# The first norm of a two-layer hybrid trunk: loads in order of need, the gain spread by products, and 22 unread products on TensorE ahead of the first transposes

## The chip, the cores and the metric

The kernel runs on one core of a Trainium2 chip. The metric is the device time of one execution in microseconds (us). The core has five instruction streams that run side by side and wait for each other by semaphores: TensorE (PE; its weight loads are shown as PEld), VectorE (DVE), ScalarE (ACT), GpSimd (POOL) and SyncE (SP), which here only issues transfers.

## What is computed

`x` has 1024 positions of 1024 channels in float32. Two layers follow each other, each with a mixer and a SwiGLU, and each of these sits between two RMS norms:

```python
def sandwich(x, g_pre, g_post, fn):
    return x + rmsnorm(fn(rmsnorm(x, g_pre)), g_post)

def even_mixer(t, layer_idx, w_in, lq1, lk1, lq2, lk2, subln, dw_w, dw_b, ln_g, ln_b, w_out, cos, sin):
    proj = t @ w_in
    y_a = diff_attention(proj[..., :3 * DIFF_WIDTH], layer_idx, lq1, lk1, lq2, lk2, subln, cos, sin)
    y_b = conformer_conv(proj[..., 3 * DIFF_WIDTH:], dw_w, dw_b, ln_g, ln_b)
    return jnp.concatenate([y_a, y_b], axis=-1) @ w_out
```

The change concerns the very start: `rmsnorm(x, l0_mix_pre)` of layer 0, the first of the projections behind it (the gated input of the convolution), and the scalar lambda of differential attention, which is made of four vectors of 64.

## The kernel before, in words

All large products are made in three terms of two rounded parts, high and low (`mm3`, lines 114 to 122): high by high, high by low, low by high, each a matmul with its own weight load. A weight unit is 128 by 1024. `unit` (L84 to L92) loads it into `raw`, ScalarE rounds it to `wh` (L89), and GpSimd subtracts to give `wl` (L91). `raw` has five buffers.

`first_norm` (L139 to L155) loads the eight blocks of 128 positions (`nt`, five buffers, L144), the gain as a transfer that repeats one line for all 128 partitions (`gpre`, L111, L150), and the first two weight units. For every block ScalarE sums the squares (`junk`, L106), GpSimd makes the inverse root (`rstd`, L97 and L98), VectorE multiplies block, root and gain (`nx`, L153), and `to_T` turns the block: eight transposes on TensorE in two groups of four (`tr`, two PSUM buffers, L181), each group rounded by ScalarE (`xt`, L183) and its low part split off by VectorE (L184). Four blocks make one half, 512 columns, of the transposed input `X`.

`conv` (L186 to L220) makes four chunks of 128 channels. For every chunk and half it forms two projections into one PSUM tile (`psc`, `proj_cm`, 24 matmuls of 512 columns each); ScalarE takes the sigmoid of the second, VectorE multiplies. Three of the eight pieces of the convolution are then made by ScalarE and GpSimd, five by VectorE (31 steps each, `psk`, L215 and L217). `qk0` makes queries and keys from the same `X` and stores them through memory. `lam` (L326 to L340) loads the four vectors, multiplies, sums, takes the exponential and scales one more gain (`sub8`).

In the program text `first_norm` comes first, then `lam`, then `conv` and `qk0`. The order in which each engine's instructions are issued is not that of the text: a scheduler places them by times that it simulates, and keeps the order fixed from then on. Transfers are all issued by SyncE in one queue in order; so is the work of ScalarE, VectorE and GpSimd.

```python
        for tb, r in enumerate(rows):
            xn = pool.tile([P, D], F32, tag="nx", name="nx", bufs=3)
            rs = self.sumsq(r)
            nc.vector.scalar_tensor_tensor(xn, r, rs, g, op0=ALU.mult, op1=ALU.mult)
            self.to_T(xn, X[tb // 4], tb % 4)
```

## Time and profile before

| | |
|---|---|
| median of 3 runs | 2328.14 us (2327.58 to 2334.51) |
| the profiled execution | 2332.52 us |
| its span, first to last instruction | 2330.1 us |
| mean granted TensorE clock | 0.968 |
| TensorE busy (matmul) | 2157.9 us, 93% of the span |
| VectorE, GpSimd, ScalarE busy | 1594.9, 1265.7, 945.2 us |
| transfers | 135 GB/s in the mean |

The profile is of one execution. Times in it count from its first instruction. The chain is the work that ended last, followed back from the end of the program: at each step to what released it. A bracket at the end of a timeline row is the time that the engine was idle before, and what ended it. A granted clock of 1.00 is TensorE's full 2.4 GHz, 0.5 is 1.2 GHz; it is recorded only from the first change on, so the pace of the products has to be looked at too in the first 30 us.

### The profile page before, as it was taken

Reading aid. Unit: us, or ns where it says so; the run is one execution under the profiler, and the core shown is the slowest. Engines: PE = TensorE matmul, PEld = TensorE weight load, DVE = VectorE, ACT = ScalarE, POOL = GpSimd, SP = SyncE. Lnnn points to the kernel's source line nnn. Section 1 sums busy time; section 2 is a strip of 40 time slices with the busy share of each in tenths; the row PEclk is TensorE's granted clock in tenths of the full one; section 3 lists DMA queues with packets and bytes.
Section 4 is the critical chain, followed back from the end, with each engine's and each line's share of the span. In section 5 each row is a group of like instructions: output and inputs, shape, how many; then the busy total and the mean of one; then the engine's idle time right before and its main releaser. Section 6 shows DMA issues by size and latency. Waiting matters only on the chain.

```text
span 2330.1 us, 27167 instructions
## 1 busy us (share of the span) xinstructions
PE 2157.9 (93%) x9684; PEld 1746.3 (75%) x9684; DVE 1594.9 (68%) x2175; ACT 945.2 (41%) x1413; POOL 1265.7 (54%) x740
## 2 busy tenths in 40 slices
PE   7999889898999999899969888999899999989987
PEld 5887677676788878687758767876688888878866
DVE  6859567689856865477884578656964444447788
ACT  5554555453222332333344346654532322234332
POOL 4997202134665556776644455421575656577674
PEclk9999999899999999899979999999999999999999
DMA  5234683243332343644542674324332323255354
GB/s 204 71 109 140 167 206 112 76 168 107 107 117 100 123 136 104 221 140 134 173 160 80 193 232 141 113 97 160 119 131 72 133 73 131 73 178 185 112 167 149
DMA packets 150662, 315.32 MB, mean 135 GB/s; under 512 B 20224, under 2 KB 43904, under 8 KB 150528
## 3 DMA queue, kind: packets, MB, share of 16 engines
q1 hardware_dynamic: 150528, 313.60, 41.4%
q8 instruction: 76, 1.25, 0.2%
q14 instruction: 58, 0.48, 0.1%
HBM read 214.39 MB, written 96.01 MB: 133 GB/s over the span
## 4 chain that ended last, share of the span: by engine, by line
PE 68%; DVE 16%; DMA 6%; issue 4%; ACT 3%; POOL 3%; SPq 0%; POOLq 0%; DVEq 0%; ACTq 0%
PE b L115 29%; PE psd L115 13%; PE psw L115 6%; PE psc L115 5%; PE psq L115 3%; PE po L115 2%; DVE hl L1253 2%; DVE acc L1271 2%; PE pss L1038 2%; PE trp L365 1%; POOL wl L1123 1%; DVE wt L1042 1%; PE pss L452 1%; DMA bm<-k_s 1%; PE psv L115 1%
## 5 line engine op out<-in xcount | busy, mean ns | idle before, releaser
L1123 POOL TENSOR_TENSOR wl<-raw,wh 128x1024 fp32r<-128x1024 f32 (+1 forms) x238 | 614.1, 2588 | 412.3 <-ACT wh L1121 399.7
L115 PE MATMUL b<-T,wh 128*128 128x512 f32 x1408 | 438.4, 392 | 2.2 <-DVE F L1172 2.2
L1121 ACT CAST wh<-raw 128x1024 fp32r<-128x1024 f32 (+1 forms) x238 | 241.9, 1023 | 433.0 <-PE b L115 251.7
L115 PE MATMUL b<-B,wh 128*128 128x512 f32 x1056 | 337.4, 400 | 15.0 <-DVE c L1163 10.5
L115 PEld LDWEIGHTS b<-T,wh 128*128 128x128 f32 x1408 | 263.8, 188 | 62.3 <-issue 2.8
L115 PE MATMUL b<-T,wl 128*128 128x512 f32 x704 | 276.4, 393 | 1.6 <-POOL wl L1123 1.6
L115 PE MATMUL psd<-wh,hh 128*128 128x512 f32 x616 | 240.6, 400 | 32.6 <-ACT hh L1252 18.9
L115 PEld LDWEIGHTS b<-B,wh 128*128 128x128 f32 x1056 | 203.0, 193 | 62.5 <-ACT B L1089 7.3
L115 PE MATMUL psd<-wl,hh 128*128 128x512 f32 x616 | 241.4, 396 | 0.0
L115 PE MATMUL psd<-wh,hl 128*128 128x512 f32 x616 | 235.2, 396 | 1.3 <-DVE hl L1253 1.3
L1271 DVE TENSOR_TENSOR acc<-acc,psd 128x512 f32<-128x512 f32 (+1 forms) x208 | 177.8, 884 | 60.1 <-PE psd L115 60.0
L115 PE MATMUL b<-B,wl 128*128 128x512 f32 x528 | 210.9, 400 | 3.6 <-POOL wl L1123 3.6
L115 PE MATMUL psw<-wh,jt 128*128 128x512 f32 x512 | 176.0, 410 | 16.0 <-ACT jt L488 9.3
L1172 DVE TENSOR_TENSOR p<-p,b 128x1024 f32<-128x1024 f32 (+1 forms) x88 | 83.5, 950 | 135.3 <-PE b L115 134.9
L1252 ACT CAST hh<-hr 128x1024 fp32r<-128x1024 f32 (+1 forms) x84 | 82.2, 979 | 223.8 <-PE psd L115 206.6
L115 PEld LDWEIGHTS psd<-wh,hh 128*128 128x128 f32 x616 | 117.2, 190 | 67.3 <-ACT hh L1252 23.9
L1253 DVE TENSOR_TENSOR hl<-hr,hh 128x1024 fp32r<-128x1024 f32 (+1 forms) x84 | 152.5, 1826 | 16.6 <-ACT hh L1252 16.6
L115 PEld LDWEIGHTS b<-T,wl 128*128 128x128 f32 x704 | 132.1, 188 | 32.7 <-POOL wl L1123 2.8
L91 POOL TENSOR_TENSOR wl<-raw,wh 128x1024 fp32r<-128x1024 f32 x48 | 122.2, 2558 | 58.4 <-ACT wh L89 58.4
L115 PEld LDWEIGHTS psd<-wh,hl 128*128 128x128 f32 x616 | 117.1, 190 | 28.9 <-DVE hl L1253 2.6
L115 PEld LDWEIGHTS psd<-wl,hh 128*128 128x128 f32 x616 | 117.5, 191 | 25.5
L1173 DVE TENSOR_TENSOR raw<-raw 128x1024 f32<-128x1024 f32 x66 | 106.7, 1617 | 41.3 <-POOL wl L1123 40.2
(386 smaller groups left out, 4314.4 us busy)
## 6 DMA issues: line engine op xcount, KB each, us to landing
raw<-in_l_gu_dram SPq DMA_DIRECT2D x96, 512.0 KB, 3.6
hr<-l_h_s SPq DMA_DIRECT2D x70, 512.0 KB, 4.1
raw<-in_l_dn_dram SPq DMA_DIRECT2D x48, 512.0 KB, 3.8
l_h_s<-F SPq DMA_DIRECT2D x66, 256.0 KB, 2.3
raw<-in_w_in_dram SPq DMA_DIRECT2D x27, 512.0 KB, 3.5
l_h_s<-c SPq DMA_DIRECT2D x44, 256.0 KB, 2.1
l_h_s<-p SPq DMA_DIRECT2D x44, 256.0 KB, 2.6
raw<-in_l_w_out_dram SPq DMA_DIRECT2D x16, 512.0 KB, 4.2
```

Source lines behind the costliest of these rows:

```text
L91: nc.gpsimd.tensor_tensor(lo, raw, hi.bitcast(F32), op=ALU.subtract)
L115: mm = lambda *t, **k: self.nc.tensor.matmul(*t, skip_group_check=go, **k)
L365: nc.tensor.transpose(tr[:, jj * P:(jj + 1) * P], Wt[:, offs[jj] + i * P:offs[jj] + (i + 1) * P], self.ident)
L452: nc.tensor.matmul(ps[:, b0:b0 + bw], Q[c][v][:, j * P:(j + 1) * P], M[c][:, b0:b0 + bw], start=v == 0, stop=v == 1)
L1038: nc.tensor.matmul(ps[:, ks], a[:, js], b[:, ks], start=first, stop=last)
L1121: nc.scalar.copy(hi[:, 0:n], r[:, 0:n])
L1123: nc.gpsimd.tensor_tensor(lo[:, 0:n], r[:, 0:n], hi[:, 0:n].bitcast(F32), op=ALU.subtract)
L1172: add = lambda o, a, b: v.tensor_tensor(o, a, b, op=ALU.add)
L1173: sub = lambda o, a, b: v.tensor_tensor(o, a, b, op=ALU.subtract)
L1252: nc.scalar.copy(hi[:, 0:n], r[:, 0:n])
L1253: v.tensor_tensor(lo[:, 0:n], r[:, 0:n], hi[:, 0:n].bitcast(F32), op=ALU.subtract)
L1271: v.tensor_tensor(dst, dst, ps, op=ALU.add)
```

## The change

- The loads are written in another order: block 0, the gain, block 1, weight unit 0, blocks 2 and 3, weight unit 1, blocks 4 to 7. All eight blocks have buffers of their own.
- The gain is loaded as one line of 4 KB, and two float32 matmuls with a row of ones spread it over the 128 partitions into PSUM. It uses one of the two large PSUM buffers, the first projection the other.
- `spin` issues 8, 6 and 8 matmuls of 128 columns in plain float32 whose results nothing reads: the first eight on the identity, six on block 0, eight on the normed block 1. They write where the projection comes to lie later.
- The projection of the first half is cut: 24 matmuls of 256 columns as soon as blocks 0 and 1 are there, and 72 after blocks 2 and 3, in place of 48 of 512.
- The low parts of the two weight units are subtracted in two pieces each.
- One-column copies make some work late: the sums of squares of blocks 6 and 7 and the weight units of chunk 1 wait for block 3's transposed tile, and `lam` is called after `qk0` and waits for the last chunk of the convolution.

```diff
--- before.py
+++ after.py
@@ -81,9 +81,11 @@
             return self.wxp.tile(shape, F32R, tag=tag, name=name)
         return self.wp.tile(shape, F32R, tag=tag, name=name, bufs=3)
 
-    def unit(self, src):
+    def unit(self, src, late=None):
         nc = self.nc
         raw = self.wp.tile([P, 1024], F32, tag="raw", name="raw")
+        if late is not None:
+            nc.scalar.copy(raw[:, 0:1], late)
         nc.sync.dma_start(raw, src)
         hi = self.wsp("wh", [P, 1024], "wh")
         nc.scalar.copy(hi, raw)
@@ -98,9 +100,11 @@
         nc.gpsimd.tensor_tensor(r, r, self.mhalf, op=ALU.pow)
         return r
 
-    def sumsq(self, a):
+    def sumsq(self, a, late=None):
         ss = self.small.tile([P, 1], F32, tag="ss", name="ss")
         junk = self.tmp.tile([P, D], BF16, tag="t", name="junk")
+        if late is not None:
+            self.nc.scalar.copy(junk[:, 0:1], late)
         if len(a.shape) == 3:
             junk = junk.rearrange("p (k c) -> p k c", k=2)
         self.nc.scalar.activation(junk, a, AF.Square, accum_out=ss)
@@ -126,33 +130,68 @@
         t = X[d // 4]
         return t[:, d % 4, 0, lo:hi], t[:, d % 4, 1, lo:hi]
 
-    def proj_cm(self, ps, W, X):
+    def proj_cm(self, ps, W, X, lo=0, hi=HALF):
         wh, wl = W
         for d in range(ND):
             c = slice(d * P, (d + 1) * P)
-            self.mm3(ps, (wh[:, c], wl[:, c]), self.xs(X, d), d == 0, d == ND - 1)
+            self.mm3(ps, (wh[:, c], wl[:, c]), self.xs(X, d, lo, hi), d == 0, d == ND - 1)
 
     def split(self, t, ps):
         self.nc.scalar.copy(t[:, 0, :], ps)
         self.nc.vector.tensor_tensor(t[:, 1, :], ps, t[:, 0, :].bitcast(F32), op=ALU.subtract)
 
     def first_norm(self, x, X, pool):
-        nc = self.nc
-        rows = []
-        for tb in range(8):
-            r = pool.tile([P, D], F32, tag="nt", name="nt", bufs=5)
-            nc.sync.dma_start(r, x[tb * P:(tb + 1) * P, :])
-            rows.append(r)
-            if tb == 3:
-                first = [self.unit(self.io["w_in0"][k]) for k in range(2)]
-            if tb == 0:
-                g = self.bcast(pool, self.io["l0_mix_pre"], "gpre")
+        nc, io = self.nc, self.io
+        row = lambda tb: nc.sync.dma_start(rows[tb], x[tb * P:(tb + 1) * P, :])
+        raw = lambda k: nc.sync.dma_start(raws[k], io["w_in0"][k])
+        rows = [pool.tile([P, D], F32, tag="nt", name="nt", bufs=8) for _ in range(8)]
+        raws = [self.wp.tile([P, D], F32, tag="raw", name="raw") for _ in range(2)]
+        line = pool.tile([1, D], F32, tag="gl", name="gl", bufs=1)
+        row(0)
+        nc.sync.dma_start(line, io["l0_mix_pre"].partition_broadcast(1))
+        row(1)
+        raw(0)
+        row(2)
+        row(3)
+        raw(1)
+        for tb in range(4, 8):
+            row(tb)
+        g = self.pp.tile([P, D], F32, tag="big", name="gpre")
+        ps = self.pp.tile([P, 2, HALF], F32, tag="big", name="psc")
+
+        def spin(n, t):
+            for _ in range(n):
+                nc.tensor.matmul(ps[:, 0, 0:P], self.ident, t[:, 0:P], start=True, stop=True)
+
+        spin(8, self.ident)
+        for c in range(2):
+            cs = slice(c * HALF, (c + 1) * HALF)
+            nc.tensor.matmul(g[:, cs], self.ones[0:1, :], line[:, cs], start=True, stop=True)
+        spin(6, rows[0])
+        W = []
+
+        def cut(k):
+            hi, lo = self.wsp("wh", [P, D], "wh"), self.wsp("wl", [P, D], "wl")
+            nc.scalar.copy(hi, raws[k])
+            for c in range(2):
+                cs = slice(c * HALF, (c + 1) * HALF)
+                nc.gpsimd.tensor_tensor(lo[:, cs], raws[k][:, cs], hi[:, cs].bitcast(F32), op=ALU.subtract)
+            W.append((hi, lo))
+
         for tb, r in enumerate(rows):
             xn = pool.tile([P, D], F32, tag="nx", name="nx", bufs=3)
-            rs = self.sumsq(r)
+            done = X[0][1][:, 0, 0, min(tb - 2, 3) * P:min(tb - 2, 3) * P + 1]
+            rs = self.sumsq(r, done if tb > 5 else None)
             nc.vector.scalar_tensor_tensor(xn, r, rs, g, op0=ALU.mult, op1=ALU.mult)
             self.to_T(xn, X[tb // 4], tb % 4)
-        return first
+            if tb in (1, 3):
+                cut(tb // 2)
+            if tb == 1:
+                spin(8, xn)
+            for k, h in {1: ((0, 0),), 3: ((0, 1), (1, 0), (1, 1))}.get(tb, ()):
+                lo = 2 * h * P
+                self.proj_cm(ps[:, k, lo:lo + 2 * P], W[k], X[0], lo, lo + 2 * P)
+        return W, ps
 
     def sandwich(self, acc, tb, res, hout, gpost, gpre, r, eng, m=None):
         nc = self.nc
@@ -189,13 +228,15 @@
         cvec = self.col(io["cvec"], 12, "cvec")
         Y = self.yp.tile([P, 4, S], F32, tag="y", name="yconv")
         for cc in range(4):
-            wa, wg = first if cc == 0 else [self.unit(io["w_in0"][2 * cc + k]) for k in range(2)]
+            wa, wg = first[0] if cc == 0 else [self.unit(io["w_in0"][2 * cc + k], X[0][1][:, 0, 0, 3 * P:3 * P + 1] if cc == 1 else None) for k in range(2)]
             cu = pool.tile([P, CW - 1 + S], F32, tag="cu", name="cu", bufs=2)
             nc.gpsimd.memset(cu[:, 0:CW - 1], 0.0)
             for hf in range(2):
-                ps = self.pp.tile([P, 2, HALF], F32, tag="big", name="psc")
-                self.proj_cm(ps[:, 0, :], wa, X[hf])
-                self.proj_cm(ps[:, 1, :], wg, X[hf])
+                ps = first[1]
+                if cc or hf:
+                    ps = self.pp.tile([P, 2, HALF], F32, tag="big", name="psc")
+                    self.proj_cm(ps[:, 0, :], wa, X[hf])
+                    self.proj_cm(ps[:, 1, :], wg, X[hf])
                 sg = pool.tile([P, HALF], F32, tag="sg", name="sg", bufs=1)
                 nc.scalar.activation(sg, ps[:, 1, :], AF.Sigmoid)
                 o = CW - 1 + hf * HALF
@@ -323,9 +364,10 @@
             nc.vector.tensor_tensor(lo, ps, hi.bitcast(F32), op=ALU.subtract)
             nc.sync.dma_start(self.v_s[tb * P:(tb + 1) * P, 1, :], lo.bitcast(F32))
 
-    def lam(self, pool):
+    def lam(self, pool, late):
         nc, io = self.nc, self.io
         lq = pool.tile([P, 4, 64], F32, tag="lq", name="lq", bufs=1)
+        nc.scalar.copy(lq[:, 0, 0:1], late)
         nc.sync.dma_start(lq, io["lams"].partition_broadcast(P))
         pr = pool.tile([P, 2, 64], F32, tag="lpr", name="lpr", bufs=1)
         nc.vector.tensor_tensor(pr, lq[:, 0:2, :], lq[:, 2:4, :], op=ALU.mult)
@@ -335,7 +377,9 @@
         nl = self.const.tile([P, 1], F32, name="neglam")
         nc.vector.tensor_tensor(nl, sm[:, 1:2], sm[:, 0:1], op=ALU.subtract)
         nc.vector.tensor_scalar(nl, nl, -0.2, None, op0=ALU.add)
-        sub = self.col(io["l0_subln"], 1, "sub8")
+        sub = self.const.tile([P, 1], F32, name="sub8")
+        nc.scalar.copy(sub, late)
+        nc.sync.dma_start(sub, io["l0_subln"])
         nc.vector.tensor_scalar(sub, sub, 0.8, None, op0=ALU.mult)
         self.neglam, self.sub8 = nl, sub
 
@@ -1349,11 +1393,11 @@
     X = [[*K.x_tiles(xp, 1), K.yp.tile([P, 4, 2, HALF], F32R, tag="y", name="xt")], K.x_tiles(xp)]
     with right("t1") as t1:
         first = K.first_norm(io["x"], X, t1)
-        K.lam(t1)
     t2s = xst.enter_context(left("t2s"))
     with right("t2") as t2:
         Yc = K.conv(X, first, t2)
         K.qk0(X, Yc, t2)
+        K.lam(t2, Yc[:, 3, 0:1])
     norms = [K.conv_norm(Yc, hf) for hf in range(2)]
     for _ in range(3):
         for n in norms:
```

**TensorE from its start.** The names: `tr` is a group of transposes, `psc` the first projection (unread products write there too), `gpre` the gain, `gl` its line, `nt` and `nx` a block before and after the norm. Before:

```order
L181 MATMUL tr<-ident,nx 128x128 x32
L115 MATMUL psc<-xt,wh 128x512
L181 MATMUL tr<-ident,nx 128x128 x4
L115 MATMUL psc<-xt,wh 128x512
L115 MATMUL psc<-xt,wl 128x512
L115 MATMUL psc<-xt,wh 128x512 x2
L115 MATMUL psc<-xt,wl 128x512
L115 MATMUL psc<-xt,wh 128x512 x2
L115 MATMUL psc<-xt,wl 128x512
```

and now:

```order
L164 MATMUL psc<-ident 128x128 x8
L164 MATMUL psc<-nt,ident 128x128 x2
L169 MATMUL gpre<-gl,ones 128x512 x2
L164 MATMUL psc<-nt,ident 128x128 x4
L220 MATMUL tr<-ident,nx 128x128 x8
L164 MATMUL psc<-nx,ident 128x128 x8
L220 MATMUL tr<-ident,nx 128x128 x8
L119 MATMUL psc<-xt,wh 128x256 x2
L119 MATMUL psc<-xt,wl 128x256
```

All four blocks of the first half were transposed ahead of the first projection; now unread products and the gain's two stand first, and a projection of 256 columns begins behind block 1. A little later, where the 72 products of that first half end and the second half (512 columns) begins, there now stands:

```order
L119 MATMUL psc<-xt,wh 128x256 x2
L119 MATMUL psc<-xt,wl 128x256
L119 MATMUL psc<-xt,wh 128x256 x2
L119 MATMUL psc<-xt,wl 128x256
L220 MATMUL tr<-ident,nx 128x128 x24
L119 MATMUL psc<-xt,wh 128x512
L220 MATMUL tr<-ident,nx 128x128 x4
L119 MATMUL psc<-xt,wh 128x512
L119 MATMUL psc<-xt,wl 128x512
```

The transposes of blocks 4 to 7 were spread among the first half's products before; 24 of the 32 are now in one piece behind them.

**ScalarE from its start**, where `junk` is a sum of squares, `wh` a weight unit rounded and `xt` a transposed group rounded. Before:

```order
L106 ACT_TABLE_LOAD
L106 ACTIVATE junk,ss<-nt 128x1024 x3
L183 CAST xt<-tr 128x4x128 x2
L106 ACTIVATE junk,ss<-nt 128x1024
L89 CAST wh<-raw 128x1024
L183 CAST xt<-tr 128x4x128
L89 CAST wh<-raw 128x1024
L183 CAST xt<-tr 128x4x128
L106 ACTIVATE junk,ss<-nt 128x1024
L183 CAST xt<-tr 128x4x128
L334 ACTIVATE lsm<-lsm 128x2
L183 CAST xt<-tr 128x4x128
```

and now:

```order
L110 ACT_TABLE_LOAD
L110 ACTIVATE junk,ss<-nt 128x1024 x2
L175 CAST wh<-raw 128x1024
L110 ACTIVATE junk,ss<-nt 128x1024 x2
L175 CAST wh<-raw 128x1024
L222 CAST xt<-tr 128x4x128
L110 ACTIVATE junk,ss<-nt 128x1024
L222 CAST xt<-tr 128x4x128
L110 ACTIVATE junk,ss<-nt 128x1024
L222 CAST xt<-tr 128x4x128 x6
L107 CAST junk<-xt 128x1 x2
L88 CAST raw<-xt 128x1 x2
```

Both weight units are now rounded ahead of the first transposed group, and the first half's groups come in one piece of six behind the fifth sum of squares.

**VectorE near the end of the convolution**, where `psk` is a step of it, `rr` and `rw` the rotation of a query or key, `sp` its split that is then stored, `lpr` to `neglam` the lambda step, `yconv` the norm of the convolution. Before:

```order
L217 SCALAR_TENSOR_TENSOR psk<-cu,dww,psk 128x512
L283 TENSOR_TENSOR rr<-rr,cos 128x512
L284 TENSOR_TENSOR rw<-rw,sin 128x512
L285 TENSOR_TENSOR rr<-rr,rw 128x512
L323 TENSOR_TENSOR vl<-psv,vh 128x512
L235 SCALAR_TENSOR_TENSOR yconv<-mu,yconv 128x512 x4
L137 TENSOR_TENSOR sp<-rr,sp 128x512
L227 TENSOR_TENSOR s_1803<-yconv 128x512
L228 TENSOR_TENSOR s_1803<-s_1803,yconv 128x512
L229 TENSOR_TENSOR s_1803<-s_1803,yconv 128x512
L323 TENSOR_TENSOR vl<-psv,vh 128x512
```

and now:

```order
L258 SCALAR_TENSOR_TENSOR psk<-cu,dww,psk 128x512
L324 TENSOR_TENSOR rr<-rr,cos 128x512
L325 TENSOR_TENSOR rw<-rw,sin 128x512
L373 TENSOR_TENSOR lpr<-lq 128x128
L383 TENSOR_SCALAR sub_1858<-sub_1858 128x1
L326 TENSOR_TENSOR rr<-rr,rw 128x512
L375 TENSOR_REDUCE lsm<-lpr 128x2
L276 SCALAR_TENSOR_TENSOR yconv<-mu,yconv 128x512 x4
L141 TENSOR_TENSOR sp<-rr,sp 128x512
L378 TENSOR_TENSOR neglam<-lsm 128x1
L364 TENSOR_TENSOR vl<-psv,vh 128x512
L379 TENSOR_SCALAR neglam<-neglam 128x1
```

The lambda multiply, the scaling of `sub` and the reduction now stand ahead of the last split `sp`; they stood among the first splits `xt` before.

## Rows read from the trace of the kernel before

**Rows 1.** Windows: busy time of each engine, granted TensorE clock, DMA share, GB/s.

```profile
60.00:200.00 140.00, 140.00 (x611) 114.66 (x610) 104.40 (x145) 80.84 (x117) 133.29 (x95) 1.00 0.27 93
200.00:230.00 30.00, 27.45 (x116) 21.28 (x115) 29.96 (x38) 13.92 (x23) 20.50 (x13) 1.00 0.47 149
```

**Rows 2.** Timeline, first 10 us: start us, us, engine, line, operation.

```profile
1.14 0.29 POOL masks.py:199 TENSOR_SCALAR_AFFINE_SELECT ident<-ident 128x128 f32<-128x128 f32 x1
...
4.18 1.06 ACT L106 ACTIVATE junk<-nt 128x1024 bf16<-128x1024 f32 x1 [2.18 <-DMA nt<-in_x_dram]
...
6.48 1.28 DVE L153 SCALAR_TENSOR_TENSOR nx<-nt,rstd,gpre 128x1024 f32<-128x1024 f32 x1 [6.48 <-DMA gpre<-in_l_mix_pre_dram]
...
7.71 1.06 ACT L106 ACTIVATE junk<-nt 128x1024 bf16<-128x1024 f32 x1 [2.39 <-DMA nt<-in_x_dram]
...
9.01 1.06 ACT L106 ACTIVATE junk<-nt 128x1024 bf16<-128x1024 f32 x1
```

**Rows 3.** Timeline, 13 to 25 us, GpSimd and VectorE.

```profile
13.75 5.64 POOL L91 TENSOR_TENSOR wl<-raw,wh 128x1024 fp32r<-128x1024 f32 x2
...
13.82 3.36 DVE L153 SCALAR_TENSOR_TENSOR nx<-nt,rstd,gpre 128x1024 f32<-128x1024 f32 x1
...
17.11 1.27 DVE L184 TENSOR_TENSOR xt<-tr,xt 128x512 fp32r<-128x512 f32 x2
...
23.08 1.29 DVE L184 TENSOR_TENSOR xt<-tr,xt 128x512 fp32r<-128x512 f32 x2 [0.57 <-ACT xt L183]
```

**Rows 4.** Timeline, 25 to 35 us, TensorE products.

```profile
25.60 1.05 PE L115 MATMUL psc<-xt,wh 128*128 128x512 f32 x2
...
26.88 1.05 PE L115 MATMUL psc<-xt,wh 128*128 128x512 f32 x2
...
33.59 0.61 PE L115 MATMUL psc<-xt,wh 128*128 128x512 f32 x2
...
34.27 0.61 PE L115 MATMUL psc<-xt,wh 128*128 128x512 f32 x2
```

**Rows 5.** The chain in order of time: start us, us, what.

```profile
29.65 0.44 PE tr L181 x4
...
41.37 0.51 PE psc L115
```

**Rows 6.** Groups of instructions, 0 to 45 us, ScalarE: busy, mean ns.

```profile
L183 ACT CAST xt<-tr 128x512 fp32r<-128x512 f32 x16 | 9.1, 585 | 13.8 <-PE tr L181 13.8
...
L89 ACT CAST wh<-raw 128x1024 fp32r<-128x1024 f32 x5 | 5.2, 1054 | 0.0
```

**Rows 7.** Windows around two pauses of TensorE, columns as rows 1.

```profile
39.40:41.40 2.00, 1.28 (x10) 0.87 (x9) 1.23 (x3) 1.17 (x2) 0.00 (x0) 1.00 0.03 8
...
237.20:240.60 3.40, 1.53 (x8) 1.00 (x7) 0.45 (x2) 2.64 (x4) 3.00 (x3) 1.00 1.04 235
240.60:244.00 3.40, 3.40 (x10) 2.63 (x9) 0.00 (x0) 0.00 (x0) 1.77 (x2) 0.51 1.05 234
```

**Rows 8.** Timeline of TensorE elsewhere: narrow products, a plain float32 product.

```profile
233.97 1.10 PE L231 MATMUL mu<-s,ones 128*128 128x512 f32 x2 [0.68 <-DVE s L229]
...
371.23 0.51 PE L115 MATMUL po<-pt,bv 128*128 128x256 f32 x3
371.58 0.60 PE L269 MATMUL rstdb<-ident,rstd 128*128 128x128 f32 x4
```

**Rows 9.** VectorE: the lambda groups (0 to 45 us), one row at 228 us.

```profile
L331 DVE TENSOR_TENSOR lpr<-lq 128x128 f32<-128x128 f32 x1 | 1.2, 1243 | 0.0
...
L333 DVE TENSOR_REDUCE lsm<-lpr 128x2 f32<-128x128 f32 x1 | 0.3, 286 | 0.0
...
L337 DVE TENSOR_SCALAR neglam<-neglam 128x1 f32<-128x1 f32 x1 | 0.2, 154 | 0.0
...
228.23 1.47 DVE L137 TENSOR_TENSOR sp<-rr,sp 128x512 fp32r<-128x512 f32 x1
```

**Rows 10.** The chain in attention: start us, us, what.

```profile
294.79 11.01 DMA bm<-k_s
```

## The prediction

> **What bounds the kernel now.** I read the windows first, then the timeline of the first 45 us by engine, then the chain that ended last. From 60 to 200 us TensorE is busy for 140.00 of 140 us, and from 200 to 230 VectorE for 29.96 of 30 [rows 1]: while the convolution and the query and key projections run, TensorE sets the pace, and at their end VectorE. All of this waits in line behind the first norm, so time gained at the front should move the whole chain forward, as long as nothing behind it is tied to a fixed moment.
>
> At the front, the first row block is there at 4.18 us, the gain's broadcast at 6.48, the next blocks at 7.71 and 9.01 [rows 2]. So 0.5 MB arrives every 1.3 us. Only when four blocks are normed, transposed and split does the first projection start, since its 512 columns are four blocks. The last split of that half is a pair of 1.29 us from 23.08, so ends at 24.37 [rows 3]. One norm multiply takes 3.36 us while a weight subtraction runs on GpSimd (two of these take 5.64); splits that read PSUM take 1.27 a pair in the same time [rows 3].
>
> The products begin slowly: from 25.60 to 26.88 three take 1.28, 0.427 each. From 33.59 to 34.27 three take 0.68, 0.227 each [rows 4]. That is half rate, then full. At 41.37 the first product of the second half of the columns starts, on the chain [rows 5]; from there TensorE hardly stops. **This moment is my yardstick: where is it after the change?**
>
> **The front, step by step.** Loads: row 0 at 4.2, then row 1, weights 0, rows 2 and 3, weights 1, rows 4 and 5, 1.3 apart: 5.5, 6.8, 8.1, 9.4, 10.7, 12.0, 13.3. The gain is one line of 4 KB between the first two and is spread by two 512-column products of float32.
>
> Such a product takes 1.10 at full clock [rows 8], an unread one of a quarter the width by that 0.27, double at half rate. Ahead of the gain's end stand ten unread and two wide ones: 4.9 us at full, 9.8 at half clock, from 1.4 us, when the identity is written [rows 2]: 6.3 to 11.2. I take 9.0, later than today's 6.48, because they begin at the low rate.
>
> VectorE then needs six norm multiplies and eight splits to finish the first half. With the gain in PSUM I take the multiply at 1.28, not 3.36, since operations with a PSUM operand were not stretched [rows 3]; a split is 0.64: 9.0 + 7.7 + 5.1 = 21.8. ScalarE is not later: weights 1 cast from 10.7 to 11.8 (1.05), then cast 0.59, squares 1.06 and their sum, cast, squares [rows 2, 6], up to 15.5. Two waits come on top. The third block's transposes stand behind thirteen products of the first quarter, which end at 18.9 and cost VectorE 1.9; the last tile costs about 0.6. **First half complete: 24.3, against 24.37.** So the rows themselves come no earlier.
>
> What is gained is work done meanwhile, and its rate. By then 24 of 96 half-width products are done. A 256-column product takes 0.117 (three from 371.23 to 371.58 [rows 8]); 72 from 23.1 cost 8.4, four transposes 0.44 [rows 5]: 32.0. But in the new order 24 transposes, six groups of four, stand behind these without a product between. There are two PSUM buffers for them, so a pair costs 0.44 + 0.59 + 0.64 and about 0.2 of handing over, 1.9. The sixth group is cast at 37.3, and the second half's first product starts there. Against 41.37: **4.1 us earlier**, if the clock is full from 17 us on.
>
> **The clock.** From 237.2 to 240.6 TensorE is busy for 1.53 of 3.40, and from 240.6 to 244.0 the granted clock reads 0.51: the 1.2 GHz level. From 39.4 to 41.4 it has 1.28 of 2.00, nearly all transposes, and the clock holds at 1.00 [rows 7]. In the new order it has almost nothing from the end of the last unread products (13.7) to the first real ones (17.4) but eight transposes, and then again from 32.0 to 37.3 some 2.6 us of transposes in 5.3. Both are longer than 39.4 to 41.4 and as thin as 237.2 to 240.6. I take one fall for each; a stretch of 3.4 at 0.427 instead of 0.227 a product loses 1.6. **Plus 3.2**; bounds 0 and 4.8 (three falls).
>
> The Trainium skill (TensorE: Matmul & The Clock Gate, Part 4: PE-mode transpose) says that transposes do not bring up the full clock as other products do. By that rule the two microseconds of transposes around 21 to 23 would cost a third fall; the row of 39.4 to 41.4, where the clock held, speaks against it.
>
> **What hides elsewhere.** The eight unread products with the second block stand ahead of its transposes: 2.2 us from 11.6, done at 13.7, while ScalarE reaches that tile only at 15.2; at half rate they end at 16.0 and would cost 0.2 to 0.8. On the SyncE queue the next chunk's weights now wait for the first half's last cast (23.6). Issued then, no more than 4.2 to land (row 0 took less from the start of the span [rows 2]) and 1.3 each for two more: 30.5, cast by 31.5, just ahead of the seven casts behind them on ScalarE at 32.0. If they are later, each microsecond is one of the front.
>
> **The lambda step** moves from the front into VectorE's full stretch. Multiply and reduction now stand ahead of the split at 228.23, which releases the last key store. The multiply is 1.24 in the trace, beside GpSimd; the reduction of the same tile 0.29; the one-column steps 0.15 [rows 9]. If the multiply alone is like the reduction: 0.29 + 0.29 + 0.15 = 0.7, at most 1.7. I take **plus 0.7**, GpSimd being near its end there. ScalarE's table load for the exponential moves ahead of it, none is added. The two small loads are issued ahead of key stores that are not ready then.
>
> **The rest.** From about 260 us attention is issued in another order here and there: a store of partial output, for example, goes behind query loads on the SyncE queue. The nearest price for one such wait is the 11.01 us on the chain for a key load [rows 10]; it may come or go. I take 0, with both ends kept.
>
> **Sum:** 2332.52 (the profiled execution: span 2330.1 and 2.4 around it) - 4.1 + 3.2 + 0.7 = 2332.3. That execution lies 4.4 above the median of the runs shown, 2328.14, so I forecast **2327.9**: no change. A measurement here can tell about 0.3%, 7.0 us.
>
> **Rivals.**
> *The clock holds.* The unread products do what their name says and the pauses don't count: 2332.52 - 4.1 + 0.7 - 4.4 = 2324.7. For it speaks 39.4 to 41.4, against it 237 to 244. Still within 0.3%. Chance 0.16.
> *Transposes count for nothing*, the skill's rule above, as a mechanism here: three falls, 2327.9 + 1.6 = 2329.5. Chance 0.10.
> *Slower: a transfer in attention.* The next head's key, query and value loads and the partial stores share one queue; if one store that the new order moves makes ScalarE, and with it TensorE, wait as the key load at 294.79 does, that is 11.0 more: 2338.9, 0.5% slower. It decides if the wait exceeds 7 us with no other work ready. For it: the chain runs through transfers there. Against: most places of the order are unchanged. Chance 0.11.
> *Faster by the same place.* The key loads leave ahead of a store and the wait of 11.0 goes: 2316.9. Chance 0.13. The order alone decides between these two; the first norm does not.
> *The unread products merely delay the gain.* All of them at half rate: gain at 11.2, first half at 26.5, the yardstick at 39.5, gain 1.9 in place of 4.1: 2330.1. Chance 0.10.
>
> **How the numbers follow.** The forecast itself has 0.40 and, by the bounds of its terms (clock 0 to 4.8, lambda 0.6 to 1.7), its own range is 2324.6 to 2330.5. The cases within 0.3% (2321.1 to 2335.1) add to 0.76, faster 0.13, slower 0.11. The range for 8 in 10 leaves out the outer parts of both transfer cases and reaches to half of what one wait can move: 2320.0 to 2336.5.
>
> **What would show it.** Right: the gain's two products end near 9; the norm multiplies read near 1.28 although GpSimd works; the first half's last split ends near 24.3; the first half-width products run at 0.2 or more and speed up later; 24 transposes from 32 on, TensorE half idle, and low granted clock within or after them; the second half's first product near 38 to 40; the split before the last key store 2 to 4 us earlier or at the same time as today. Wrong: multiplies of 3.4 with the gain in PSUM, a second half that starts later than 41.4, ScalarE waiting for weights in front of the seven casts, or a front and an attention stage whose shifts against before differ by more than 5 us.

## The result, and the profile after

The changed kernel takes 2344.99 us (median of 4 runs, 2342.87 to 2346.42) against 2328.16 for the kernel before: ratio 1.0062, 95% interval 1.0042 to 1.0082. It is 0.6% slower; the forecast of no change, and its range up to 2336.5, were wrong. The profiled execution took 2343.59 us, 11.1 more than that of before (2332.52).

**Where the time went.** I compare the start of each instruction with that of its counterpart before, and take the median over a stretch of 10 us of the old time. This shift is -0.2 us at 200, -1.0 at 280, +5.6 between 330 and 340, +13.0 at 370, +11.5 at 460 and +11.7 at the end. So front and lambda step bring a little, and attention of layer 0 loses 12.5 us between 280 and 460; behind it the shift moves up and down by 2 to 3 us and ends where it was. Both traces are of single executions, and those of the kernel before alone range from 2324.47 to 2339.67 us in the runs of e15 to e17, so a difference of a few us between two shifts shows nothing by itself. The full stretches of [rows 1] are there as before:

```profile
60.00:200.00 140.00, 140.00 (x611) 114.67 (x610) 104.33 (x145) 80.63 (x117) 133.35 (x94) 1.00 0.27 93
200.00:230.00 30.00, 26.08 (x109) 19.85 (x108) 29.31 (x43) 15.20 (x27) 19.62 (x13) 1.00 0.46 149
```

**The front**, timeline of the changed kernel (columns as rows 2; `x4` are the gain's two products, each a pair of matmuls), with the lambda step at its end:

```profile
6.05 3.78 PE L169 MATMUL gpre<-gl,ones 1*128 1x512 f32 x4
...
9.93 3.76 DVE L185 SCALAR_TENSOR_TENSOR nx<-nt,rstd,gpre 128x1024 f32<-128x1024 f32 x3 [9.93 <-PE gpre L169]
...
18.88 0.39 PE L119 MATMUL psc<-xt,wh 128*128 128x256 f32 x1 [1.91 <-DVE xt L223]
...
21.04 0.59 ACT L222 CAST xt<-tr 128x512 fp32r<-128x512 f32 x1 [3.57 <-PE tr L220]
...
26.17 0.69 DVE L223 TENSOR_TENSOR xt<-tr,xt 128x512 fp32r<-128x512 f32 x1 [0.83 <-ACT xt L222]
...
34.43 1.03 PE L220 MATMUL tr<-ident,nx 128*128 128x128 f32 x8
...
35.12 1.28 DVE L185 SCALAR_TENSOR_TENSOR nx<-nt,rstd,gpre 128x1024 f32<-128x1024 f32 x1 [4.60 <-issue]
...
41.10 0.50 PE L119 MATMUL psc<-xt,wh 128*128 128x512 f32 x1 [0.68 <-ACT xt L222]
...
224.27 0.28 DVE L373 TENSOR_TENSOR lpr<-lq 128x128 f32<-128x128 f32 x1
...
225.13 0.27 DVE L375 TENSOR_REDUCE lsm<-lpr 128x2 f32<-128x128 f32 x1
...
227.72 0.67 DVE L141 TENSOR_TENSOR sp<-rr,sp 128x512 fp32r<-128x512 f32 x1
```

The first half of `X` is complete at 26.86 (26.17 and 0.69), and the yardstick, the first product of the second half, stands at 41.10 where it was 41.37 [rows 5].

**Attention.** Here the first output projection of the convolution's half fills gaps between the heads (`w_out_first`, L542): groups of 12 products into `psw`, a ScalarE copy to `pe`, and a store of 256 KB to `part`. A store has landed when its data are written; only then is its buffer free. PSUM and SBUF have one buffer each, and the stores share SyncE's queue with the 256 KB loads of the next head's queries and keys. The chain of before, two places (columns as rows 5):

```profile
305.87 7.51 DMA part<-pe
...
313.40 0.59 ACT pe L503
...
314.04 3.06 PE psw L115 x12
...
341.18 6.57 DMA part<-pe
...
347.83 0.59 ACT pe L503
```

and the chain of the changed kernel:

```profile
307.43 7.50 DMA part<-pe
314.95 0.59 ACT pe L547
315.59 5.48 PE psw L119 x12
...
347.25 7.93 DMA part<-pe
355.20 0.59 ACT pe L547
355.84 5.49 PE psw L119 x12
```

A store behind six head loads lands after 6.6 to 7.9 us in both kernels. What differs is what TensorE has to do meanwhile, and the rate of the products behind the pause: at the first place 12 products take 3.06 us there and 5.5 here. The windows show it, before:

```profile
300.00:320.00 20.00, 16.66 (x78) 13.54 (x79) 13.65 (x48) 9.64 (x26) 0.31 (x1) 0.86 0.85 229
340.00:360.00 20.00, 17.59 (x91) 14.73 (x90) 13.00 (x44) 10.09 (x25) 1.01 (x1) 0.91 0.40 105
```

and after:

```profile
300.00:320.00 20.00, 13.84 (x49) 10.69 (x50) 11.52 (x41) 7.49 (x20) 0.00 (x0) 0.67 0.82 208
340.00:360.00 20.00, 12.98 (x58) 9.92 (x57) 10.43 (x37) 8.96 (x22) 1.32 (x2) 0.88 0.75 180
```

TensorE's own rows give the pauses (in brackets). Before, the longest two there:

```profile
314.04 0.50 PE L115 MATMUL psw<-wh,jt 128*128 128x512 f32 x1 [2.66 <-ACT pe L503]
...
348.98 0.50 PE L115 MATMUL psw<-wh,jt 128*128 128x512 f32 x1 [2.41 <-ACT jt L488]
```

After, two longer ones, and ScalarE's wait that causes the first:

```profile
314.95 0.59 ACT L547 COPY pe<-psw 128x512 f32<-128x512 f32 x1 [6.67 <-DMA part<-pe]
...
315.59 0.79 PE L119 MATMUL psw<-wh,jt 128*128 128x512 f32 x1 [4.67 <-ACT pe L547]
...
355.84 0.79 PE L119 MATMUL psw<-wh,jt 128*128 128x512 f32 x1 [5.17 <-ACT pe L547]
```

After 2.66 us idle the group takes 3.06, full rate; after 4.67 and 5.17 it takes 5.48 and 5.49, near half rate. The kernel before is not free of this: behind its 2.41 us the granted clock is 0.66 while the group is made. ScalarE stands in the copy until the landing, with casts and exponentials behind it that VectorE and TensorE wait for. In SyncE's queue the late store stands behind six loads:

```profile
341.49 0.54 SPq L434 DMA_DIRECT2D bl<-q_s  x1
...
347.25 0.33 SPq L548 DMA_DIRECT2D part<-pe  x1
```

The waits between 296 and 420 us say the same in sums: ScalarE for `part` 9.1 us before (3 times) and 17.1 after (5), TensorE for `pe` 2.7 (once) and 11.3 (4).

### The profile page after: what moved, and what is told of

Read it like the earlier page. It is cut to its first block, busy times and chain, and to the rows that moved or that the text cites. A ratio compares the mean times of both kernels' runs of the same rounds, so it can differ in the third digit from the quotient of the medians.

```text
span 2341.8 us, 27381 instructions
## 1 busy us (share of the span) xinstructions
PE 2166.8 (93%) x9780; PEld 1755.7 (75%) x9780; DVE 1577.2 (67%) x2175; ACT 946.7 (40%) x1419; POOL 1259.9 (54%) x742
## 4 chain that ended last, share of the span: by engine, by line
PE 67%; DVE 16%; DMA 6%; issue 4%; POOL 3%; ACT 3%; SPq 1%; POOLq 0%; DVEq 0%; ACTq 0%
PE b L119 29%; PE psd L119 13%; PE psw L119 6%; PE psc L119 5%; PE psq L119 3%; PE po L119 2%; DVE hl L1297 2%; PE pss L1082 2%; DVE acc L1315 2%; DMA part<-pe 1%; PE trp L409 1%; POOL wl L1167 1%; PE psu L119 1%; PE pss L496 1%; PE psv L119 1%
## 5 line engine op out<-in xcount | busy, mean ns | idle before, releaser
L119 PE MATMUL b<-B,wh 128*128 128x512 f32 x1056 | 335.2, 398 | 13.9 <-DVE c L1207 10.2
L119 PE MATMUL psw<-wh,jt 128*128 128x512 f32 x512 | 178.0, 414 | 24.9 <-ACT pe L547 11.3
L1297 DVE TENSOR_TENSOR hl<-hr,hh 128x1024 fp32r<-128x1024 f32 (+1 forms) x84 | 150.3, 1800 | 14.3 <-ACT hh L1296 14.3
L93 POOL TENSOR_TENSOR wl<-raw,wh 128x1024 fp32r<-128x1024 f32 x46 | 114.3, 2496 | 52.1 <-ACT wh L91 52.0
L119 PEld LDWEIGHTS psw<-wh,jt 128*128 128x128 f32 x512 | 97.8, 194 | 53.1 <-ACT pe L547 14.6
```

What stands on the lines that cost most here:

```text
L93: nc.gpsimd.tensor_tensor(lo, raw, hi.bitcast(F32), op=ALU.subtract)
L119: mm = lambda *t, **k: self.nc.tensor.matmul(*t, skip_group_check=go, **k)
L1297: v.tensor_tensor(lo[:, 0:n], r[:, 0:n], hi[:, 0:n].bitcast(F32), op=ALU.subtract)
```

## The experiments

All in one table. A pin is a line that fixes the order of two instructions for the scheduler. "Front" is the shift against before at 200 us, "attention" the shift at 460 less that at 280, "end" that of the last 40 us, all of one profiled execution; the ratio is that of the timed runs to runs of before on the same chip.

| run | us | ratio, interval | front | attention | end |
|---|---|---|---|---|---|
| the change | 2344.99 | 1.0062 (1.0042-1.0082) | -0.2 | +12.5 | +11.7 |
| e1 lambda step alone | 2343.86 | 1.0059 (1.0042-1.0076) | 0.0 | +11.2 | +14.3 |
| e2 change, 8 unread | 2336.43 | 1.0030 (1.0019-1.0042) | +0.1 | -0.2 | +4.7 |
| e3 change, none unread | 2344.57 | 1.0064 (1.0048-1.0081) | +0.9 | +8.4 | +11.9 |
| e4 change, 8, 6, 4 unread | 2332.82 | 1.0014 (1.0004-1.0023) | -2.0 | +4.4 | +2.5 |
| e5 before, no stores | 2321.80 | 0.9957 (0.9939-0.9974) | 0.0 | -14.6 | -10.6 |
| e6 change, no stores | 2322.70 | 0.9962 (0.9943-0.9981) | +5.1 | -9.6 | -3.9 |
| e7 before, own queue | 2333.50 | 1.0012 (0.9996-1.0028) | -0.8 | -0.6 | +1.5 |
| e8 change, own queue | 2333.95 | 1.0013 (0.9997-1.0029) | +0.4 | +0.2 | -0.7 |
| e9 change, three pieces | 2345.91 | 1.0069 (1.0056-1.0082) | +2.9 | +8.9 | +13.9 |
| e10 before, three pieces | 2332.79 | 1.0006 (0.9997-1.0016) | +0.3 | +2.7 | +4.1 |
| e11 e4 with three pieces | 2344.20 | 1.0062 (1.0050-1.0074) | +0.7 | +8.6 | +12.3 |
| e12 change, one store ahead | 2337.60 | 1.0032 (1.0022-1.0043) | +1.2 | +10.2 | +8.7 |
| e13 before, that store behind | 2330.11 | 0.9997 (0.9983-1.0010) | -0.8 | -5.2 | -5.4 |
| e14 e4, that store ahead | 2337.70 | 1.0032 (1.0021-1.0043) | +2.2 | -0.4 | +2.9 |
| e15 change, one group pinned | 2336.59 | 1.0024 (1.0011-1.0037) | +2.0 | +3.3 | +2.6 |
| e16 e1, same pin | 2334.54 | 1.0016 (1.0003-1.0028) | +0.3 | +5.4 | +1.6 |
| e17 e4, pinned | 2332.44 | 1.0006 (0.9992-1.0021) | -0.5 | -0.3 | -2.0 |
| e18 change, two pins | 2335.24 | 1.0019 (1.0007-1.0031) | +5.1 | -1.2 | +2.9 |

**Which part of the change? (e1 to e4)** The lambda step alone, with the late waits of the change, on the old front; then the change with other numbers of unread products.

```diff
 e1, in the kernel before
-        K.lam(t1)
+        K.lam(t2, Yc[:, 3, 0:1])
 e2: only the first spin; e3: no spin; e4:
-                spin(8, xn)
+                spin(4, xn)
```

> The kernel before, with the lambda step alone moved behind the queries and keys. Its front is issued as before; in attention TensorE's order comes out the same as in the changed kernel, to the last product. If the order in attention makes the loss: 2340 to 2346, with the shift against before near zero up to 260 us and 12 to 15 us behind 400. If the front of the change makes it (first norm, unread products, clock): 2327 to 2330. If the lambda step itself costs (its wait or its table load in VectorE's full stretch): slower too, but with the shift already there at 240 to 260 us.

> The changed kernel with the first 8 of the 22 unread products only. TensorE's order in attention comes out as before but for 7 places. If the order in attention makes the loss: 2325 to 2330, although all of the front and the moved lambda step are kept. If the lambda step or the new front makes it: 2340 to 2347. If the missing 14 products matter for the clock, the first projection starts at half rate and the front is 1 to 3 us later than in the changed kernel.

> The changed kernel without any unread product. TensorE's order in attention is that of the changed kernel. If the order in attention makes the loss: 2340 to 2347 again. If the unread products make it, 2328. What the unread products bring at the front is read at 60 to 200 us: if they keep the clock up, this kernel is 2 to 4 us later there than the changed one; if not, within 1 us.

> The changed kernel with 18 unread products in place of 22 (four with the second block, not eight). TensorE's order in attention is a third one, neither that of before nor that of the changed kernel; otherwise nothing changes. If the order in attention makes the loss, the time differs from the changed kernel's by more than 4 us, either way: between 2322 and 2340. If anything else makes it: 2343 to 2346, since four products of 0.27 us are all that goes.

e1 has the old front to the tenth of a microsecond and nearly the whole loss. The scheduler gives it the attention order of the changed kernel, from a step of five small VectorE instructions that now ends at 229 us, some 70 us ahead of where the orders part for good. e2 gets the order of before but for 7 places on TensorE, and is 0.3% off instead of 0.6%: between its two expectations. In its profile front and attention are level with before, and the 4.7 us of the end come behind 460; why is open. So the new front is not needed for the loss, and it and the lambda step both tip the same order. In e3 the front is 1.2 us later than in the change's profile, but 0.9 lies inside the range of the profiles with all 22 unread products (last section): a gain from them is not shown.

**Are the stores the cause? (e5 to e8)** Without them (their share of the result left out), or from GpSimd's queue.

```diff
 e5, e6
-            nc.sync.dma_start(self.part[tb * P:(tb + 1) * P, cs], t)
...
-            nc.sync.dma_start(a, self.part[tb * P:(tb + 1) * P, :])
+            nc.sync.dma_start(a, self.io["x"][tb * P:(tb + 1) * P, :])
 e7, e8
-            nc.sync.dma_start(self.part[tb * P:(tb + 1) * P, cs], t)
+            nc.gpsimd.dma_start(self.part[tb * P:(tb + 1) * P, cs], t)
```

> The kernel before, without the 16 stores of partial output in attention (the first half of the output projection is left out of the result; the later load reads the input in their place, the same bytes). The attention order that comes out of it is a third one, the same as in the run with the changed kernel's front. Theory (ScalarE and TensorE wait in attention for these stores to land, behind the head loads of the same queue): ScalarE's 9 us and TensorE's 3 us of such waits are gone, and the stretch from 290 to 440 us is 5 to 12 us shorter: 2316 to 2324 us. Rival (the order itself, which products stand where, sets the time, the stores are covered): within 3 us of before.

> The changed kernel, without the same 16 stores (same part of the result left out). Theory: the loss of 13 us between 290 and 380 us is gone with the stores, and the run is 0 to 2 us below the kernel before without stores (what the front and the lambda step bring). Rival (the new front or the later lambda step hurt attention by something else, such as the clock or the loads of the first head): still 8 us or more above it.

> The kernel before, with the 16 stores issued by GpSimd, so in another queue than the head loads. Theory: a store lands about 2 to 3 us after its issue also when head loads run, ScalarE's waits for it stay under 4 us each, and the kernel takes 2318 to 2326 us. Rival (the stores share the transfer engines with the loads, so another queue changes nothing; and GpSimd pays for issuing): landing still 5 to 8 us at the head loads, 2328 to 2340 us.

> The changed kernel with the stores in GpSimd's queue. Theory: no loss in attention; 0 to 2 us below the kernel before with the same queue, and below 2328. Rival: 5 us or more above the kernel before with the same queue, since its order still differs from it in some 250 places.

Without stores both kernels fall to the same time, 0.4% under before: the stores, with the order that comes with them, cost even the kernel before 8 us (2329.84 in these runs), and where the attention order is alike the change costs nothing. Another queue is no remedy: the longest landing was 8.2 and 8.5 us, and the gain that I expected did not come. The two kernels were again equal, although by the expectation of e8 their orders differ in some 250 places: so a difference in that many places does not cost time by itself.

**Is it the wait for a landing as such? (e9 to e11)** Three buffers of 256 columns instead of one of 512, with TensorE's order nearly kept.

```diff
-            t = pool.tile([P, HALF], F32, tag="pe", name="pe", bufs=1)
-            nc.scalar.copy(t, ps)
-            nc.sync.dma_start(self.part[tb * P:(tb + 1) * P, cs], t)
+            for q in (0, 256):
+                t = pool.tile([P, 256], F32, tag="pe", name="pe", bufs=3)
+                nc.scalar.copy(t, ps[:, q:q + 256])
+                nc.sync.dma_start(self.part[tb * P:(tb + 1) * P, cs.start + q:cs.start + q + 256], t)
```

> The changed kernel with the copy out of the output projection made in pieces of 256 columns with three buffers, so that a copy waits for the store of three pieces before it, not for the last one. TensorE's order in attention stays that of the changed kernel up to the eighth output group, so the order is kept and only the wait is loosened; the copies are 32 of about 0.35 us in place of 16 of 0.59. Theory (the wait for the landing is what the changed order costs): ScalarE's waits for landings go from 17 us to under 6, the shift against before at 380 us from 16 us to under 6, and the kernel takes 2322 to 2332 us, at least 10 less than the changed kernel. Rival (the order costs by itself: products late for their operands, the clock): the shift at 380 us stays over 10 us, 2338 us or more.

> The kernel before with the same three pieces; its order in attention differs from that of before in some 50 places. Theory: its 9 us of waits shrink too, 2320 to 2328 us; the changed kernel with three pieces is within 4 us of it. Rival: no gain over before (2328 to 2333 us), and the changed kernel with three pieces is still 8 us or more above it.

> The changed kernel with 8, 6 and 4 unread products, whose front was 2 us ahead of before, and three pieces. If the wait for landings is what is left to gain, this is the fastest: 2318 to 2326 us. If the two don't add, it lies where before lies, 2326 to 2332 us.

My theory missed, in all three runs. e10 gained nothing (1.0006). In e9 the waits for landings shrank from 17.1 to 12.2 us and the time did not move, since the three that were left are the long ones:

```profile
ACT pe L548 <- DMA part<-pe: 12.2, 3, 5.0
```

Three buffers of half the size put off a wait by half a group; a landing of 7.3 us outlasts that. Why the third order became 11 us worse with pieces (e11) stays open.

**Is it one store's place in the queue? (e12 to e14)** The sixth store ahead of the last head's six loads, as before has it, or behind (e13 names two loads more). `K.stores` and `K.heads` hold the transfers in the order of the program text; the line orders their issue and adds no wait. The lines that fill these lists are left out here and below.

```diff
 e12, e14
+    for h, c, x in K.heads[38:44]:
+        tc.add_manual_dep(x.ins, K.stores[5].ins.name, info, reason="order")
 e13, in the kernel before
+    for x in (x for h, c, x in K.heads[36:44]):
+        tc.add_manual_dep(K.stores[5].ins, x.ins.name, info, reason="order")
```

> The changed kernel with one place in SyncE's queue pinned as before has it: the sixth store of partial output is issued ahead of the six loads of the last head (two of the low queries, two of the high, two of the keys), not behind them. TensorE's order stays the changed one up to the eighth output group. Theory (this store, which stands behind 1.5 MB of loads in the changed order, blocks ScalarE's copy and the exponentials behind it and makes TensorE idle until it runs at half clock): the pause at 347 to 356 us and the half-rate output group behind it are gone, the shift against before at 380 us falls from 16 to 4 to 9 us, and the kernel takes 2332 to 2340 us. Rival (the other 250 places of the order cost it): 2342 us or more, shift at 380 us 12 or more.

> The kernel before with the same store pinned behind these six loads, as the changed kernel has it; TensorE's order stays that of before up to the seventh output group. Theory: a landing of 7 us or more at about 345, an output group at half rate behind it, a shift of 5 to 10 us at 380, and 2333 to 2341 us. Rival: within 3 us of before.

> The changed kernel with 8, 6 and 4 unread products (front 2 us ahead of before; 2332.8 us without the pin) and the store ahead of the loads. Theory: the half-rate output group at 354 us goes, worth 2 to 5 us: 2326 to 2331 us, at or below before. Rival: 2332 us or more.

Not by itself. In e12 the store goes ahead of the six loads and still lands only after 8.4 us. The run is 0.3% off instead of 0.6%, inside its expectation, but its profile still has both pauses (4.13 and 3.12 us, the groups behind them 4.33 and 4.46), and at 380 us it is no earlier than the change. In e13 the landing of 7.3 us, a pause of 3.36 and a group of 5.05 at 347 came as expected, and yet it lost nothing: before idles there itself, 2.41 us with a slow group behind, and at 460 the shift of e13 is -6.2. e14 missed and came out worse than e4.

**Is it the order, and which places of it? (e15 to e18)** Before, TensorE's third output group stands behind the twelfth of the 24 matmuls of head 0's second value product; in the changed order behind the ninth. In the lines, `K.groups` are the output groups, `K.pvs` the value products, `K.copies` the ScalarE copies, counted from 0.

```diff
 e15, e16: third group behind the twelfth product
+    tc.add_manual_dep(K.groups[2][0].ins, K.pvs[1][11].ins.name, info, reason="order")
 e17: sixth group behind the second group of transposes of head 1 (tr21)
+    tc.add_manual_dep(K.groups[5][0].ins, tr21.ins.name, info, reason="order")
 e18: that, and ScalarE's second copy behind the fifth cast (cast14)
+    tc.add_manual_dep(K.copies[1].ins, cast14.ins.name, info, reason="order")
```

> The changed kernel with one line added: TensorE issues the third output group in attention only behind the twelfth of 24 products of head 0's second value product (it stood behind the ninth). With this alone the scheduler's order in attention falls back to that of before but for 15 places on TensorE, while front and lambda step stay as changed. Theory (the loss is the changed order in attention and nothing else of the change): the shift against before at 460 us goes from 11.5 to between -2 and 4 us, and the kernel takes 2326 to 2334 us. Rival (front or lambda step hurt attention whatever the order): shift at 460 us 9 or more, 2340 us or more.

> The kernel before with the lambda step alone moved late, and the same third output group pinned: TensorE's order in attention is then that of before but for 6 places. Theory: 2326 to 2333 us, 11 us or more below the lambda step alone without the pin (2343.9). Rival: 2340 us or more.

One line brings the order of before back in all but 15 (e15) and 6 places (e16) on TensorE, and by the ratios 9 to 10 us of the time. Both runs still miss their expectations, by 2.6 and 1.5 us. The second pause is back at the size of before (e15, columns as rows 1: 17.74 of 20 busy where the change has 12.98), the first is not:

```profile
300.00:320.00 20.00, 13.55 (x53) 10.35 (x53) 10.19 (x40) 7.79 (x23) 1.01 (x1) 0.70 0.96 240
340.00:360.00 20.00, 17.74 (x91) 14.99 (x90) 13.38 (x46) 11.53 (x29) 1.32 (x2) 0.91 0.74 189
```

The timeline of e16 shows the difference that is left: it is on ScalarE. The copy now stands ahead of a cast, and TensorE waits for that cast, 5.01 us, instead of for the copy:

```profile
314.80 0.59 ACT L508 COPY pe<-psw 128x512 f32<-128x512 f32 x1 [6.52 <-DMA part<-pe]
315.29 0.59 ACT L373 CAST pt<-trp 128x512 fp32r<-128x512 f32 x1
...
315.93 0.79 PE L116 MATMUL po<-pt,bv 128*128 128x512 f32 x1 [5.01 <-ACT pt L373]
```

> The changed kernel with 8, 6 and 4 unread products and the sixth output group pinned behind the second group of transposes of head 1, which brings its order near that of before (94 places on TensorE, the queue of transfers but for 2). Its front was 2 us ahead of before. If front and order add: 2325 to 2330 us, at or below before. If attention takes the gain back: 2331 us or more.

> The changed kernel, whole, with two lines that pin order: ScalarE's second copy out of the output projection goes behind the fifth cast of head 0's second value product (it stood behind the third), and the sixth output group behind the second group of transposes of head 1. Theory (the loss is two pauses: TensorE idle about 5 us at 311 to 316 because ScalarE stands in that copy with casts behind it, and the one at 347 to 356; each followed by a group at half rate): both are gone, the shift against before is under 4 us at 320 and between -3 and 4 us at 460, and the kernel takes 2327 to 2334 us, 11 us or more below the changed kernel. Rival (a pause of that size comes back at another place): shift at 460 us 6 or more, 2336 us or more.

With ScalarE's place moved as well, the changed kernel loses nothing in attention (-1.2 us, where it lost 12.5), with front and lambda step kept. So the loss is shown to be the order in attention for its greater part: e1 has it with that order alone, and the pins take away, by the ratios, some 10 of 14 us. Where it arises is seen in the shift of TensorE's instructions alone: in the change it grows by 5.5 us from 300 to 330 and by 6.5 from 330 to 370, the two pauses; in e18 by 2.9 and by -2.3, since the second pause is now 2.15 us at full rate, where before has 2.41 and a slow group. The first pause, expected gone, is still 3.38 us, with a group of 4.62 behind it. Which of the moved instructions make the pauses is argued, not shown: the two lines of e18 move much more than two places (its order comes near that of e17). The median of e18 is 10 us under the change and 0.2% above before; in this profile the front is 5.1 us late, which the last section takes up. Both numbers miss the expectation by 1 us. e17 equals before (1.0006), but its front was 0.5 us ahead and not 2, so the sum of front and order that I hoped for did not come. None of the kernels that compute everything beats the kernel before.

## Why the prediction was wrong

- **The step that failed** is "From about 260 us attention is issued in another order here and there [...] I take 0, with both ends kept". It measured +12.5 us. The rival of the transfer had a price near that, 11.0 us, and named ScalarE's and TensorE's wait for a store. That the price is near is luck: it is a key load's time, and the store that the new order moves is not what decides (e12, e13); the landing is as long before, 7.5 us, and what differs is how much work is issued ahead of the wait. Its weight of 0.11 rested on "most places of the order are unchanged". One TensorE group, three products earlier, goes with some 250 changed places: pinning it alone brought all but 15 back (e15).
- "The order alone decides between these two; the first norm does not": right, and shown by e1 and, for the greater part of the loss, by e18. But order was treated as a coin between two ends around zero. The kernel before held a good draw: of the orders that came up here with the stores in SyncE's queue, none was faster, and most were slower by 0.1 to 0.7%.
- **Front -4.1:** measured -0.3, without the loss by the clock that was to come on top. The sum of both terms, -0.9, came near by luck: one was 3.8 us too good, the other 3.2 too bad. The gain's products ended at 9.83 (forecast 9.0), and three multiplies took 3.76 although GpSimd worked beside them, so the gain in PSUM did what was said. But the first half was complete at 26.86, not 24.3: the cast at 21.04 waits 3.57 us for transposes that stand behind 13 products, and this happens for three groups, not one. And the last six groups took 6.7 us from 34.43, not 5.3: the eighth multiply (35.12) needs one of three `nx` buffers, which the first four of those transposes free. Its row names no releaser; this is read from the program and the times. I had counted the PSUM buffers and not these.
- **Clock +3.2:** nothing in the profiled execution, whose products run at 0.12 from 18.88 on. It is a draw too: the falls came in other executions of this front (below), worth up to 5 us.
- **Transposes count for nothing** (rival, 0.10, after the Trainium skill, TensorE: Matmul & The Clock Gate, Part 4): not in this execution. From 34.43 to 41.10 TensorE had only transposes, in pieces of about 1.1 us with pauses up to 1.69, and the product at 41.10 is a full-rate one. In e15 and e18 the granted clock did fall there, to 0.50 and 0.74 in 40 to 44 us, in and behind the same 24 transposes; the runs show both.
- **Lambda +0.7:** the three instructions take 0.28, 0.27 and 0.14, as estimated, but the split behind them comes at 227.72, 0.5 earlier [rows 9], and e1 alone costs nothing up to 280. VectorE's order changed around them.
- **Against the list of what would show it:** 24 transposes behind the products, multiplies of 1.28 with GpSimd busy: right. First half complete near 24.3: wrong, 26.86. The second half's first product near 38 to 40: wrong, 41.10. First products at half rate: wrong here, right in e18. "A front and an attention stage whose shifts differ by more than 5 us" was named as the sign of a wrong forecast; that is what came.

## What to carry over

Where a scheduler orders a kernel, a small edit can re-deal a distant stage; compare the two orders there and ask of every moved instruction in front of a long wait how much work its engine, and the engines that follow it, have left during that wait. Price such a draw by the longest pause it can open and by the rate of the products behind it, and give it a weight near that of the whole forecast. To price an edit, pin the order of the stages it should not touch, and look whether the pins brought all of it back: here they did not quite.

## What the runs showed that was not expected

**A pause can cost more than itself.** TensorE idle for 1.66 (e13) and 2.66 us was followed by an output group of 3.06; for 3.27, 3.38 and 5.09 (e17, e18, e2) by one of 4.61 or 4.62; for 4.67 and 5.17 by 5.48 and 5.49. So each of these five longer pauses cost 1.5 to 2.4 us on top of itself. The shorter ones go both ways: behind 2.53 us in e14 the group took 4.62 at a granted clock of 0.63, behind 2.26 us in e17 3.33 at 1.00, two products of another kind included. And a pause counts only against what the other kernel has at that place: e2 is 4.1 us behind at the first and wins 2.4 back at the second.

**The same front runs at two rates.** In e18 the gain's four matmuls took 1.98 us, in the changed kernel's profile 3.78, so the full rate came earlier. The unread products were then done at 12.8 instead of 15.5 us, TensorE stood idle up to the next transposes, the clock fell, and the first real products ran at half rate: its front is 5.1 us late. Timeline of e18, and its granted clock (columns as rows 1):

```profile
5.29 1.98 PE L171 MATMUL gpre<-gl,ones 1*128 1x512 f32 x4
...
10.47 2.32 PE L166 MATMUL psc<-nx,ident 128*128 128x128 f32 x16
14.26 0.66 PE L222 MATMUL tr<-ident,nx 128*128 128x128 f32 x4 [1.47 <-DVE xt L225]
...
18.80 0.58 PE L121 MATMUL psc<-xt,wh 128*128 128x256 f32 x1 [1.91 <-DVE xt L225]
```

```profile
14.00:18.00 4.00, 1.40 (x9) 1.00 (x9) 3.13 (x4) 2.79 (x7) 3.16 (x6) 1.00 0.92 329
18.00:21.40 3.40, 2.60 (x12) 2.60 (x13) 1.34 (x3) 0.00 (x0) 0.00 (x0) 0.51 0.02 5
```

Over the seven profiles with all 22 unread products the shift at 200 us lies between -0.2 and +5.1; over the six with the old front between -0.8 and +0.3. In e18 the unread products ended too early to fill the gap, and over these profiles the front is less steady with them. How often each rate comes was not measured.
